# A hybrid decoder layer: the stick-breaking projections in pairs of units by seven block products instead of eight

## The chip, the cores and the metric

The kernel runs on one core of one Trainium2 chip. The metric is device time in microseconds of one execution; two runs of the kernel before took 2079.24 and 2085.99 us, their median is 2082.61 us. Five engines work on their own queues, each in the order in which its instructions stand: TensorE (PE, with its weight loads as PEld), VectorE (DVE), ScalarE (ACT), GpSimd (POOL) and SyncE (SP, which issues nearly all transfers).

## The reference, cut to what matters

Sequence 1024, model width 2048, float32, one layer:

```python
h = rmsnorm(h_res, g_pre[i])
u = h @ w_in[i]                       # 2048 x 7184, split into nine groups of columns
(gq, gk, gv, g_gate, g_lr, sq, sk, sv, s_gate) = jnp.split(u, offsets, axis=-1)
log_a = jax.nn.log_sigmoid(g_lr @ w_a2[i] + b_a[i]) / GLA_TAU
o_gla = gla_chunked(...)              # 4 heads, keys 128 wide, values 256 wide, chunked recurrence
o_gla = rmsnorm(o_gla, g_gla_head[i]).reshape(B, S, D_GLA) * jax.nn.silu(g_gate)
o_sb = stick_breaking(heads(sq), heads(sk), heads(sv))   # 8 heads, 128 wide, strictly causal
o_sb = o_sb.transpose(0, 2, 1, 3).reshape(B, S, D_SB) * jax.nn.silu(s_gate)
mix = jnp.concatenate([o_gla, o_sb], axis=-1) @ w_out[i]
h_res = h_res + rmsnorm(mix, g_post[i])
gate = jax.nn.sigmoid(h_res @ w_ple_gate[i] + b_ple_gate[i])
h_res = h_res + gate * (p[i] @ w_ple_proj[i])
```

In stick-breaking, per query t and earlier key s, A[t,s] = sigmoid(z_ts) times the product of (1 - sigmoid(z_tj)) over the keys j between s and t; z is query times key over sqrt(128).

## The kernel before

**Splitting.** Every operand of a large product is split into two parts, `hi` (an ACT copy that rounds to the matmul's type) and `lo` (a DVE subtraction), and a product is three matmuls: hi with x-hi, lo with x-hi, hi with x-lo. All activations lie with the model dimension on the 128 partitions and tokens along the free axis, in two halves of 512 tokens (`hf` 0 and 1). The normed input x stands split in SBUF as 16 blocks of 128 rows for each half (`x_act[hf][k]`, tiles `ah`, `al`), stored two blocks wide in 16 places.

**Stages.** (1) Load and split x; the first two units run beside it. (2) A unit is 128 columns of `w_in`: `dense` loads four weight tiles of 128x512 (`wload`, `L126`: `raw` by the SP queue, then `split`), and runs 16 blocks x 3 matmuls x 2 halves = 96 matmuls of 128x512 into two PSUM banks called `dn`; at the end the result is taken out on DVE times the row norm `rstd` (`u<-dn,rstd`, `v<-dn,rstd`). First come the 16 units of the four GLA heads, then the 24 units of the eight stick-breaking heads (key, query, value of each). (3) The gate columns (`w_gate`), the output product (`w_out`) and the last gate (`w_g`) are each done as a 2x2 block product by seven block products instead of eight, with sums of x and of the weights; sums of x (`S1` to `S4`) are made in `x_sums`, put to memory and loaded back when a place in SBUF comes free.

**Small products.** `small_product` is a block product: 8 blocks of x by one 1024x128 block of weights, 24 matmuls, from two half loads of weights of 128x512. In the kernel before 16 of them run between the last unit and the wide stages, which use `product` with weights loaded 128x1024.

**Background work.** The chunked recurrence (`gla`) and the stick-breaking attention (`sb`) are generators. After every 6 matmuls of the dense work `step()` moves the generators on; `rate` and `pace` say how often. `sb` makes per head twelve score rows: matmuls into `z`, two sigmoids on ACT (`X<-z`, `E<-z`), the causal mask on POOL (`affine_select`, line 597), a running product on DVE (`L603`), a product (`L608`), an ACT copy and a transposing transfer by SP (`X<-E`, then `E<-X`), eight steps (`L1`) later a DVE copy that regroups (`L618`, `v<-E`) and a split (`s`), and eight steps (`L2`) later the product with the values into banks `o` and `t`. Values are turned the same way (`turn`) and split.

**Order.** The code is written in one order; a scheduler with priorities sets the order on each queue (`high_priority(offset=700)` draws the weights ahead, 300 the evacuations). All waits are semaphores that the scheduler derives from the tiles; a pool's number of buffers limits how far ahead a load can stand. Weights have `raw` 2 and `hi`, `lo` 4 buffers each; one pair of `hi`, `lo` feeds 24 matmuls in `dense` and 12 in `small_product`.

Of the kernel before, what the change touches and what calls it, by code (L numbers as in the profile page):

```python
# [18 lines left out]
P = 128  # L19
# [17 lines left out]
def unit_offsets():  # L37
    offs = []
    for h in range(GLA_HEADS):
        offs += [OFF_GK + P * h, OFF_GQ + P * h, OFF_GV + 2 * P * h, OFF_GV + 2 * P * h + P]  # L40
    for h in range(SB_HEADS):
        offs += [OFF_SK + P * h, OFF_SQ + P * h, OFF_SV + P * h]
    return offs
# [4 lines left out]
RATE_SB = 0.9  # L48
W3 = 4
V_MID, V_END, VW = ("X", "X"), ("E", "E"), 3  # L50
L1, L2, PERIOD = 8, 8, 5
W = 2 * HT
# [3 lines left out]
RATE_TAIL = 1.1  # L56
LAST_11 = 4
PACE_QKV, PACE_TAIL = 15, 4
# [3 lines left out]
def layer(ctx, tc, xT, w_in, w_gate, w_lr, w_a2, b_a, g_pre, g_head, w_out, g_post,  # L62
# [17 lines left out]
    w_open = tc.tile_pool(name="w", bufs=4, side="right")  # L80
# [40 lines left out]
    lo_eng = [V]  # L121

    def wload(src):
        n = src.shape[-1]
        with tc.high_priority(offset=700):
# [4 lines left out]
            dma(raw[:, :n], src)  # L130
# [34 lines left out]
    pace = [0, PACE_QKV]  # L165
# [45 lines left out]
    pair = {}  # L211
    acc = {}
    lr_ps = {0: ps("t"), 1: ps("o")}
    first = [{hf: ps("dn") for hf in HALVES} for _ in range(2)]
    with tc.tile_pool(name="start", bufs=1) as sp:
# [21 lines left out]
        for q in range(4):  # L237
            w = [wload(w_in[n, q]) for n in range(2)]
            for kk in range(4):
                k = 4 * q + kk  # L240
                sl = slice(kk * P, (kk + 1) * P)
                for hf in HALVES:
# [7 lines left out]
                    x_act[hf][k] = (ah, al)  # L250
                    A.activation(ah, raw, AF.Copy, scale=gpre_s[:, k:k + 1])  # L251
# [27 lines left out]
    keep = ctx.enter_context(tc.tile_pool(name="keep", bufs=1, reuse_waits="tile"))  # L279
    with tc.tile_pool(name="att", bufs=1, reuse_waits="tile") as ap:  # L280
        BUFS = {"u": 12, "E": 2, "X": 2, "s": 2, "q": 1, "v": 1, "b": 1, "st": 2, "o": 1, "eb": 4}
        GLA_BUFS = {"a2": 1, "a2h": 1, "a2c": 1, "lr": 1, "kt": 1, "o2": 1, "mask": 1}
        SB_BUFS = {"E2": 2, "s2": 2, "X2": 1}
        own = [tc.tile_pool(name="gla", bufs=1, reuse_waits="tile")]
        own.append(own[0].__enter__())

        def to_sb():
            own[0].__exit__(None, None, None)
            own[0] = tc.tile_pool(name="sb", bufs=1, reuse_waits="tile")
            own[1] = own[0].__enter__()  # L290

        def at(tag, shape=(P, HT), dt=F32):
            pool, bufs = (ap, BUFS[tag]) if tag in BUFS else (own[1], {**GLA_BUFS, **SB_BUFS}[tag])
# [10 lines left out]
        gap(const, 224)  # L304
# [15 lines left out]
        def evac_turned(dst, parts):  # L320
            def go(hf, p):
                vt = at("v")
                V.tensor_tensor(vt, p, rstd[hf], op=ALU.mult)
                if parts == 1:
                    dst[hf] = at("u")
                else:
                    dst[hf] = (at("u", dt=F32R), at("u", dt=F32R))
                urgent.append(turn(vt, dst[hf], parts))
# [10 lines left out]
        def turn(vt, dst, parts):  # L339
            w = turn_by_dma(vt, HT, V_MID[parts - 1], V_END[parts - 1])  # L340
            for _ in range(VW):
                yield 1
            full = dst if parts == 1 else at("o")
# [405 lines left out]

# [633 lines left out]
```

## Time and profile before

| | |
|---|---|
| median of two runs | 2082.61 us |
| span of the profiled execution, first to last instruction | 2075.1 us |
| PE busy | 2060.6 us (99%), 9712 matmuls |
| DVE busy | 1481.9 us (71%) |
| ACT busy | 874.1 us (42%) |
| POOL busy | 112.0 us (5%) |
| transfers | 352.81 MB, mean 170 GB/s |
| granted TensorE clock | 1.000 |

The page gives the profiled execution by its span; a time of its own stands nowhere, so the median is set beside the span: 7.5 us lie between them. In the page's groups of instructions the first number is the busy time in us, the second the mean of one instruction in ns; then follows the idle time of the engine just before these instructions and what ended most of it. A window's row gives, for each engine, the busy time in that stretch and the number of instructions in brackets, then the granted clock, the mean busy share of the 16 DMA engines and the rate. The share of busy time is no bound by itself: matmuls overlap.

### The profile page before, as it was taken

The numbers are of one execution on the slowest core, as the hardware profiler recorded it, in microseconds if no ns is written. First come the engines' busy times: TensorE is split into PE (matmuls) and PEld (weight loads), VectorE is DVE, ScalarE is ACT, GpSimd is POOL, SyncE is SP. The second block draws the span as 40 slices with busy tenths as digits, with TensorE's granted clock in tenths as the row PEclk, the third lists the DMA queues.
The fourth block names the chain that finished last, engine by engine and source line by source line (L and its number), as shares of the span: only waits on it lengthen the run. The fifth ranks groups of instructions, "written<-read, shape, count | busy, mean of one in ns | idle before, by whom it ended". The sixth has DMA issues, their size and how long they took to land.

```text
span 2075.1 us, 26732 instructions
## 1 busy us (share of the span) xinstructions
PE 2060.6 (99%) x9712; PEld 1706.3 (82%) x9712; DVE 1481.9 (71%) x2243; ACT 874.1 (42%) x1390; POOL 112.0 (5%) x229
## 2 busy tenths in 40 slices
PE   9999999999999999999999999999999999999998
PEld 6788888888888888888888788888888888888887
DVE  8657777676766676666567677788778687886765
ACT  7333334333454554555447423344233334423322
POOL 4100000000011011101001000000000000000000
PEclk9999999999999999999999999999999999999999
DMA  6222222232243344443326798888978486886752
GB/s 219 69 67 78 82 78 82 66 87 67 62 126 88 106 107 108 113 105 97 84 79 156 213 328 295 306 298 303 335 283 269 163 313 229 307 292 210 243 190 98
DMA packets 229700, 352.81 MB, mean 170 GB/s; under 512 B 124336, under 2 KB 129344, under 8 KB 229568
## 3 DMA queue, kind: packets, MB, share of 16 engines
q1 hardware_dynamic: 228960, 349.00, 53.2%
q10 hardware_dynamic: 576, 2.10, 0.3%
q8 instruction: 76, 1.25, 0.2%
q14 instruction: 56, 0.46, 0.1%
q0 software_dynamic: 32, 0.01, 0.0%
HBM read 249.85 MB, written 73.92 MB: 156 GB/s over the span
## 4 chain that ended last, share of the span: by engine, by line
PE 90%; DVE 3%; DMA 3%; issue 2%; ACT 1%; SPq 0%; POOL 0%; DVEq 0%; ACTq 0%; POOLq 0%
PE dn L101 79%; PE z L101 5%; PE t L101 3%; PE o L101 3%; DMA E<-X 1%; DMA xraw<-xT 1%; DVE rstd L235 0%; DMA u<-xT 0%; DVE lo L114 0%; DVE al L252 0%; DVE X L603 0%; DVE E L608 0%; DMA raw<-w_gate 0%; ACT hi L113 0%; ACT ah L251 0%
## 5 line engine op out<-in xcount | busy, mean ns | idle before, releaser
L101 PE MATMUL dn<-ah,hi 128*128 128x512 f32 x1408 | 561.7, 399 | 2.3 <-ACT u L736 1.9
L101 PE MATMUL dn<-ah,lo 128*128 128x512 f32 x1408 | 549.6, 390 | 0.2 <-DVE lo L114 0.2
L101 PE MATMUL dn<-al,hi 128*128 128x512 f32 x1408 | 549.4, 390 | 0.0
L101 PE MATMUL dn<-ah,wl 128*128 128x512 f32 x1216 | 473.4, 389 | 0.0
L101 PE MATMUL dn<-al,wh 128*128 128x512 f32 x1216 | 473.1, 389 | 0.0
L101 PE MATMUL dn<-ah,wh 128*128 128x512 f32 x1216 | 473.1, 389 | 0.0
L101 PEld LDWEIGHTS dn<-ah,hi 128*128 128x128 f32 x1408 | 265.0, 188 | 60.2 <-issue 3.6
L101 PEld LDWEIGHTS dn<-al,hi 128*128 128x128 f32 x1408 | 264.3, 188 | 57.6 <-DVE al L252 0.4
L101 PEld LDWEIGHTS dn<-ah,lo 128*128 128x128 f32 x1408 | 265.2, 188 | 48.1 <-DVE lo L114 0.5
L113 ACT ACTIVATE wh<-wr 128x1024 fp32r<-128x1024 f32 x152 | 159.4, 1055 | 268.1 <-PE dn L101 168.9
L101 PEld LDWEIGHTS dn<-ah,wl 128*128 128x128 f32 x1216 | 228.3, 188 | 48.7 <-DVE wl L114 1.2
L101 PEld LDWEIGHTS dn<-al,wh 128*128 128x128 f32 x1216 | 228.3, 188 | 47.3
L101 PEld LDWEIGHTS dn<-ah,wh 128*128 128x128 f32 x1216 | 228.3, 188 | 47.3
L114 DVE TENSOR_TENSOR wl<-wr,wh 128x1024 fp32r<-128x1024 f32 x152 | 185.0, 1218 | 7.0 <-ACT wh L113 6.7
L113 ACT ACTIVATE hi<-raw 128x512 fp32r<-128x512 f32 x192 | 119.7, 625 | 153.4 <-PE dn L101 137.9
L114 DVE TENSOR_TENSOR lo<-raw,hi 128x512 fp32r<-128x512 f32 x192 | 134.7, 703 | 59.6 <-ACT hi L113 59.5
L333 ACT ACTIVATE X<-E 128x256 uint16<-128x256 uint16 (+2 forms) x96 | 81.0, 844 | 142.8 <-DVE E L608 70.2
L603 DVE TENSOR_TENSOR_SCAN X<-X 128x128 f32<-128x128 f32 (+2 forms) x96 | 97.8, 1019 | 14.4 <-POOL X L597 13.0
L618 DVE COPY v<-E 128x512 uint16<-128x512 uint16 (+1 forms) x160 | 64.1, 430 | 48.5 <-DMA E<-X 45.3
L114 DVE TENSOR_TENSOR s<-v,s 128x512 fp32r<-128x512 f32 (+1 forms) x82 | 52.6, 642 | 61.1 <-ACT s L113 60.9
L884 DVE TENSOR_TENSOR wr<-wr,wr 128x1024 f32<-128x1024 f32 x48 | 58.7, 1223 | 49.4 <-issue 15.1
L881 DVE TENSOR_TENSOR wr<-wr,wr 128x1024 f32<-128x1024 f32 x48 | 58.7, 1224 | 47.5 <-DMA wr<-w_g 34.0
(246 smaller groups left out, 2292.6 us busy)
## 6 DMA issues: line engine op xcount, KB each, us to landing
raw<-w_in SPq DMA_DIRECT2D x160, 256.0 KB, 2.7
wr<-w_g SPq DMA_DIRECT2D x64, 512.0 KB, 4.4
wr<-w_out SPq DMA_DIRECT2D x56, 512.0 KB, 4.8
wr<-w_gate SPq DMA_DIRECT2D x40, 512.0 KB, 5.2
g_d<-wr SPq DMA_DIRECT2D x32, 512.0 KB, 3.8
wr<-g_d SPq DMA_DIRECT2D x32, 512.0 KB, 4.5
ar<-h_d SPq DMA_DIRECT2D x28, 512.0 KB, 4.9
ar<-og_d SPq DMA_DIRECT2D x25, 512.0 KB, 5.3
```

Source lines behind the costliest of these rows:

```text
L101: PE.matmul(o, lhsT, rhs, start=start, stop=stop)
L113: A.activation(hi, src, AF.Copy)
L114: (eng or V).tensor_tensor(lo, src, f(hi), op=ALU.subtract)
L333: A.activation(pl.rearrange("p (two n) -> p two n", two=2), src.bitcast(U16)[:, :2 * n].rearrange("p (n two) -> p two n", two=2), AF.Copy)
L603: V.tensor_tensor_scan(rev, rev, rev, initial=kq[:, n:n + 1], op0=ALU.mult, op1=ALU.bypass)
L618: V.tensor_copy(to[:, :, :m, j], w[:, :, 2 * g:2 * g + m])
L881: V.tensor_tensor(dst, a, b, op=ALU.add)
L884: V.tensor_tensor(dst, a, b, op=ALU.subtract)
```

## The change

The 24 stick-breaking units become 12 pairs of 128 columns each. For a pair, the 2048 x 256 weights are seen as 2x2 blocks of 1024 x 128, and x as 2x2 blocks of 1024 rows by 512 tokens; the four results (two units x two halves) come from seven block products in place of eight. The sums of x are made earlier (`x_sets`, from the third unit on), stored already split, and whole sets of x are loaded back into the four places of x during the stage (`load_set`, `swap`). The sums of weights are formed on DVE in a chain tile (`ch<-ch,raw`). The results are no longer taken out of PSUM into SBUF for the heads: they are copied to a tile `pt`, written to memory (`kqv_d`) by SP for a first group of products and added to it by POOL transfers with `accum_op=add` for the second, and each head loads its keys, queries and values when it starts. They are stored without the row norm; keys and values are multiplied by `rstd` on loading, and the queries' norm goes into the scale of the sigmoids (`rq`, for which eight small transposes are added). The gate columns are done the same way: `by_waves` gives four of the seven products, and a last loop the other three, in place of the former gate stages. Half of the regrouping copies of the attention (`L618`) go from DVE to ACT (`regroup`). The output product and the last gate stay as they are.

```diff
-RATE_SB = 0.9
+RATE_SB = 1.0
+Q1, V0, V1, NEXT_Q, NEXT_K = 8, 3, 14, 30, 33
-LAST_11 = 4
-PACE_QKV, PACE_TAIL = 15, 4
+RATE_TAIL = 1.0
+PACE_X, PACE_SET = 5, 2
+ACCUMULATE, REGROUP = False, 1
+BATCHES = ((0, 1, 2), (3, 4, 5), (6, 7))
...
+        def regroup(j, dst, src):
+            if j >= REGROUP:
+                A.activation(dst, src, AF.Copy)
+            else:
+                V.tensor_copy(dst, src)
...
+            def fetch(h, what, hf):
+                if (h, what, hf) not in fetched and h in sb_ready:
+                    fetched[h, what, hf] = t = at("u")
+                    dma2(t, kqv_d[h][what][hf])
...
-                    split(kh[hf], kl[hf], kp[hf])
+                    raw = take(h, 0, hf)
+                    kh[hf], kl[hf] = at(tag, dt=F32R), at("u", dt=F32R)
+                    V.tensor_tensor(raw, raw, rstd[hf], op=ALU.mult)
+                    split(kh[hf], kl[hf], raw)
...
+            tp = ps("z")
+            for c in range(4):
+                PE.transpose(ch(tp, c), ch(rstd[hf], c), idn)
...
+        def load_set(name, slot):
+            got = []
+            for i, (hf, kp) in enumerate(home[slot]):
+                pair = act_wide(hf, kp)
+                for d, t in zip(sx_d[name][i], pair):
+                    with tc.issue_after(last_load[0]):
+                        dma2(f(t), d)
+                    yield 1
+                got.append(pair)
+            sets[name] = parts(got)
...
+        def wt(tag, bufs, dt=F32):
+            return w2.tile([P, HT], dt, tag=tag, name=nm(tag), bufs=bufs)
+        def begin(i, src):
+            chain[i] = []
             for q in range(2):
+                t = wt("ch", 6)
+                last_load[0] = dma(t, part(src, q)).ins
+                chain[i].append(t)
+
+        def extend(i, src):
+            for q, t in enumerate(chain[i]):
...
+                raw = wt("raw", 2)
+                last_load[0] = dma(raw, part(src, q)).ins
+                V.tensor_tensor(t, t, raw, op=ALU.add)
+
+        def small_product(name, i, p):
+            while name not in sets:
+                assert beside
+                advance(beside)
+            a = sets[name]
+            for q in range(2):
+                with tc.high_priority(offset=700):
+                    hi, lo = wt("hi", 3, F32R), wt("lo", 3, F32R)
+                    split(hi, lo, chain[i][q])
...
+        def onto(dst, t, first):
+            if first:
+                dma2(dst, t)
+            else:
+                G.dma_start(dst, t, accum_op=ALU.add)
+
+        def kept(p, scale=1.0):
+            t = wt("pt", 4)
+            A.activation(t, p, AF.Copy, scale=scale)
+            return t
...
+        def by_waves(items, first, weight, at_d, swaps, mid=None):
+            upper, fifth = {}, {}
+            names = ("A11", "s1", "S2", "A22")
+            blocks = ((0, 0), (0, 1), (1, 1), (1, 0))
...
+                with early():
+                    (begin if s == 0 else extend)(i, weight(i, *blocks[s]))
+                p = ps("dn")
+                small_product(names[s], i, p)
+                if x == len(items) - 1 and names[s] in swaps:
+                    swap(names[s], swaps[names[s]])
+                with soon():
+                    if s == 0:
+                        upper[i] = kept(p)
+                        onto(at_d("c11", i), upper[i], first)
+                    elif s == 1:
+                        fifth[i] = p
+                    else:
+                        V.tensor_tensor(upper[i], p, upper[i], op=ALU.add)
+                    if s == 2:
+                        t = wt("pt", 4)
+                        V.scalar_tensor_tensor(t, fifth[i], -1.0, upper[i], op0=ALU.mult, op1=ALU.subtract)
+                        for m in ("c12", "c22"):
+                            if at_d(m, i) is not None:
+                                onto(at_d(m, i), t, first)
+                    elif s == 3:
+                        onto(at_d("c21", i), upper[i], first)
+
+        def by_stages(items, first, weight, at_d, swaps):
+            for m in ((2, 3, 7) if first else (3, 7, 2)):
+                name = {2: "A12", 3: "S4", 7: "S3"}[m]
...
+        to_2, to_1 = {"A11": "S4", "s1": "S3", "S2": "A12"}, {"A12": "A11", "S4": "s1", "S3": "S2"}
+        def sb_items(stage, first, b, swaps={}):
+            stage(range(3 * b, 3 * b + 3), first, lambda i, kh, nh: w_sb[i, kh, nh], sb_d, swaps)
+            pace[1] = PACE_SET
+            if not first:
+                sb_ready.update({2 * b: True, 2 * b + 1: True})
+                rate[1] = RATE_SB
+
+        sb_items(by_waves, True, 0)
+        sb_items(by_waves, True, 1, to_2)
+        sb_items(by_stages, False, 0)
+        sb_items(by_stages, False, 1)
+        sb_items(by_stages, True, 2)
+        sb_items(by_stages, True, 3, to_1)
+        sb_items(by_waves, False, 2)
+        sb_items(by_waves, False, 3)
...
+        for js in BATCHES[:-1]:
+            gate_batch(js)
...
+    gate_batch(BATCHES[-1], {"A11": "A12", "s1": "S3", "S2": "S4"}, to_wide)
...
+            p = product(need("A12"), w2_)
+            gate(j, 0, p, part(p11, j), add)
...
+            p = product(need("S3"), w7)
+            gate(j, 1, p, v(j), lambda z, p, c: sub(z, c, p))
+            gate(8 + j, 1, p, u(j), add)
+            p = product(need("S4"), w3)
+            gate(8 + j, 0, p, u(j), add)
```

Two places of the order show what moves. The first is DVE in the middle of the attention. In the kernel before: `lo` is a weight part, `X` the running product, `E` the score row, `v` and `s` the regrouped weights of the attention, `st` a query, `u<-u,b` a key's split.

```order
L603 SCALAR_TENSOR_TENSOR X_7818<-X_7818 128x512
L114 TENSOR_TENSOR st_8017<-u_7716,st_8017 128x128
L608 TENSOR_TENSOR E_7819<-E_7819,X_7818 128x512
L603 SCALAR_TENSOR_TENSOR X_7839<-X_7839 128x512
L114 TENSOR_TENSOR lo_8081<-raw_8079,hi_8080 128x512
L608 TENSOR_TENSOR E_1634_7840<-E_1634_7840,X_7839 128x512
L114 TENSOR_TENSOR u_7980<-u_7426,b_7979 128x512
```

Of the kernel after, DVE in the attention, during a wave of block products; `ch` is a chain of weights, `pt` a result on its way to memory:

```order
L122 TENSOR_TENSOR lo_9118<-ch_8687,hi_9117 128x512
L657 SCALAR_TENSOR_TENSOR X_9028<-X_9028 128x256
L895 TENSOR_TENSOR ch_8687<-ch_8687,raw_9229 128x512
L895 TENSOR_TENSOR ch_8527<-ch_8527,raw_9332 128x512
L953 TENSOR_TENSOR pt_8609<-dn_8973,pt_8609 128x512
L122 TENSOR_TENSOR lo_9171<-ch_8612,hi_9170 128x512
L956 SCALAR_TENSOR_TENSOR pt_9071<-dn_8804,pt_8609 128x512
L661 COPY eb_9038<-X_9028 128x1
L662 TENSOR_TENSOR E_2006_9029<-E_2006_9029,X_9028 128x256
```

Between the attention's instructions there stood one weight split; now there stand splits, chain sums and sums of results. The second place is POOL at the same spot. Before, only the masks of the score rows and the ones beside them:

```order
L595 MEMSET X_7505 128x1
L597 AFFINE_SELECT X_7470<-X_7470 128x128
L597 AFFINE_SELECT E_7471<-E_7471 128x128
L597 AFFINE_SELECT X_7505<-X_7505 128x128
L597 AFFINE_SELECT E_1563_7506<-E_1563_7506 128x128
```

After, on POOL, with the adding transfers of the results:

```order
L922 DMA kqv_d<-pt_9071 128x512 x2
L649 MEMSET X_9250 128x1
L922 DMA kqv_d<-pt_9222 128x512 x2
L651 AFFINE_SELECT X_9250<-X_9250 128x128
L651 AFFINE_SELECT E_9251<-E_9251 128x128
```

Adding transfers now stand ahead of masks in POOL's queue.

More of the change, by code (lines that the diff above doesn't have):

```diff
@@ L303, in layer @@
         pick = const.tile([P, 2], F32, name="pick")
-        gap(const, 224)
+        rq = [const.tile([P, 8], F32, name=f"rq{i}") for i in range(2)]
+        gminus = const.tile([P, KT], F32, name="gminus")
+        gap(const, 96)
+        V.tensor_scalar(gminus, gpre_s, -1.0, None, op0=ALU.mult)
         V.tensor_copy(pick, sel[:, P:P + 2])
@@ L662, in layer @@
         sb_ready = {}
+        kqv_d = [[[dram.tile([P, HT], F32, name=f"kqv{h}{i}{hf}_d") for hf in HALVES] for i in range(3)]
+                 for h in range(SB_HEADS)]
         def norm_first(hf):
@@ L716, in x_sums, with swap @@
                 keep("S4", k, a12)
+                store_plain()
                 yield 1
+        def load_set(name, slot):
[3 more added lines that the diff above has]
+                for d, t in zip(sx_d[name][i], pair):
+                    with tc.issue_after(last_load[0]):
+                        dma2(f(t), d)
+                    yield 1
+                got.append(pair)
+            sets[name] = parts(got)
+        def swap(old, new):
+            sets.pop(old, None)
+            slot = place.pop(old)
+            place[new] = slot
+            beside.append(load_set(new, slot))
@@ L808, in keep_11 @@
-        def keep_11(j, new):
-            def go(p):
-                t = new()
-                V.tensor_tensor(t, p, part(u1_s[j // 2], j) if j < 6 else u1_s[j], op=ALU.add)
-                dma2(part(c11_d[j // 2], j), t)
-            return go
-        while beside:
-            advance(beside)
-        rate[1], pace[1] = RATE_TAIL, PACE_TAIL
-        beside.append(x_set("S2", 1))
-        for j in range(8):
-            small_product(x_act[0][:8], w_gate[0, 0, j], keep_u1(j))
-        while beside:
-            advance(beside)
@@ new lines, in layer, with gate_batch @@
+        sb_items(by_waves, True, 0)
[6 more added lines that the diff above has]
+        sb_items(by_waves, False, 3)
+        g_d = {m: [dram.tile([P, W], F32, name=f"{m}g{i}_d") for i in range(4)] for m in ("c11", "c12", "c21")}
+        def gate_batch(js, swaps={}, mid=None):
+            by_waves(js, True, lambda j, kh, nh: w_gate[kh, nh, j],
+                     lambda m, j: part(g_d[m][j // 2], j) if m in g_d else None, swaps, mid)
@@ L835, in layer @@
[L835 to L849 removed]
+        att_open.__exit__(None, None, None)
@@ L858, in state @@
         def state(which):
-            return [act.tile([P, W], F32, tag=f"{which}0_{kp}", name=nm("st")) for kp in range(4, 8)]
+            return [act.tile([P, W], F32, tag=f"{which}{hf}_{kp}", name=nm("st")) for hf, kp in home[0]]
         def to_slot(s, i, raw):
@@ L1069, in layer @@
-        drain()
-        job(fill("A11", 0, plain(og_d[0])))
-        for j in range(8):
-            with ahead():
-                w = wsplit(wload2(w_gate[1, 1, j]))
-            p = product(sets["S4"], w)
-            gate(8 + j, 0, p, v(j))
-        drain()
+                w2_ = wsplit(wload2(w_gate[1, 0, j]))
+                t3, b22 = wload2(w_gate[0, 1, j]), wload2(w_gate[1, 1, j])
+                add(t3, t3, b22)
+                w7, w3 = wsplit(t3), wsplit(b22)
+                if j % 2 == 0:
+                    with tc.issue_after(last_load[0]):
+                        dma2(st_v[j // 2], g_d["c21"][j // 2])
+                        dma2(st_u[j // 2], g_d["c12"][j // 2])
```

355 lines of the change are left out of this document (193 added, 162 removed).

## Prediction

> **What bounds the kernel now.** First the page's head and its chain of what ended last.
>
> ```profile
> span 2075.1 us, 26732 instructions
> PE 2060.6 (99%) x9712; PEld 1706.3 (82%) x9712; DVE 1481.9 (71%) x2243; ACT 874.1 (42%) x1390; POOL 112.0 (5%) x229
> ...
> PE 90%; DVE 3%; DMA 3%; issue 2%; ACT 1%; SPq 0%; POOL 0%; DVEq 0%; ACTq 0%; POOLq 0%
> ```
>
> PE has 90% of the chain. What one of its matmuls is worth has to be read twice: from the groups, and from the same chain in order of time, where the dense product runs undisturbed.
>
> ```profile
> L101 PE MATMUL dn<-al,hi 128*128 128x512 f32 x1408 | 549.4, 390 | 0.0
> ...
> 1172.74 344.35 PE dn L101 x1519
> ```
>
> One matmul lasts 390 ns, but 1519 in a row take 344.35 us, which is 226.7 ns each: they overlap, and only the interval counts for the span. The page "Perfetto Trace Analysis" of the Trainium skill, section "Identifying the Most-Contended Engine", says the same of busy time: for TensorE it is no measure of the way to the limit, because the instructions are pipelined. By busy time the 288 matmuls below would be worth 112 us, by the interval 65; the trace decides for the interval.
>
> Then the windows, by stage: the GLA heads, the attention, its last 50 us, the passage to the wide stages, a wide stretch, and the one with the most DVE work.
>
> ```profile
> 150.00:550.00 400.00, 399.44 (x2072) 333.16 (x2071) 290.81 (x579) 154.06 (x266) 14.37 (x13) 1.00 0.26 75
> 570.00:1150.00 580.00, 578.97 (x2809) 487.73 (x2807) 387.63 (x746) 308.92 (x607) 65.97 (x189) 1.00 0.42 107
> 1100.00:1150.00 50.00, 50.00 (x243) 42.21 (x242) 39.14 (x75) 34.47 (x70) 7.19 (x19) 1.00 0.63 163
> 1150.00:1180.00 30.00, 27.09 (x130) 22.05 (x129) 20.12 (x34) 15.46 (x27) 0.00 (x0) 1.00 0.69 204
> 1200.00:1500.00 300.00, 300.00 (x1325) 248.40 (x1324) 233.13 (x228) 104.89 (x107) 0.00 (x0) 1.00 0.88 310
> 1750.00:1800.00 50.00, 50.00 (x223) 41.40 (x222) 45.07 (x48) 23.13 (x29) 0.00 (x0) 1.00 0.91 312
> ```
>
> PE is the bound in every stage. In the attention DVE is busy for 67% and ACT for 53%: there is room, and the question is how much of it the change uses up. The passage shows the first loss: 2.9 us of 30.
>
> **The change, part by part.**
>
> *Matmuls.* The order holds 7872 matmuls into `dn` before and 7584 now: 24 units of 96 are 2304, 12 pairs of 7 products of 24 are 2016. 288 x 0.2267 us = 65.3 us, all on the path. The eight transposes of the norm cost between 0.06 us each (a quarter of a 512-column interval) and their full duration in the nearest row:
>
> ```profile
> L492 PE MATMUL t<-c,E 128*128 128x128 f32 x32 | 4.9, 274 | 0.3 <-DVE E L390 0.3
> ```
>
> that is 0.5 to 2.2 us; I take 1.
>
> *DVE in the attention.* Its work has to fit beside a shorter PE. In the new order the first score row stands at `dn` matmul 2346 (before: 1968), the last product with values at 4224 (4122). In the window above 733 of 2809 matmuls are not `dn`: (580 - 2076 x 0.2267) / 733 = 0.149 us each. The new stretch is then 1878 x 0.2267 + 768 x 0.149 = 540 us of PE, the old one 603. For DVE the interval counts too, not the duration:
>
> ```profile
> L114 DVE TENSOR_TENSOR lo<-raw,hi 128x512 fp32r<-128x512 f32 x93 | 63.8, 686 | 29.0 <-ACT hi L113 28.8
> L603 DVE TENSOR_TENSOR_SCAN X<-X 128x512 f32<-128x512 f32 x47 | 60.4, 1285 | 7.1 <-POOL X L597 6.0 <-ACT X L592 1.0
> L618 DVE COPY v<-E 128x512 uint16<-128x512 uint16 x123 | 54.3, 461 | 44.9 <-DMA E<-X 41.8 <-ACT X L333 1.8
> ...
> 844.35 0.68 DVE L608 TENSOR_TENSOR E<-E,X 128x512 f32<-128x512 f32 x1
> 844.95 0.68 DVE L114 TENSOR_TENSOR u<-u,b 128x512 fp32r<-128x512 f32 x1
> 845.56 0.69 DVE L114 TENSOR_TENSOR u<-u,q 128x512 fp32r<-128x512 f32 x1
> 846.16 0.28 DVE L114 TENSOR_TENSOR st<-u,st 128x128 fp32r<-128x128 f32 x1
> ...
> 848.36 0.65 DVE L618 COPY v<-E 128x512 uint16<-128x512 uint16 x2
> ```
>
> Back to back, an operation of 0.69 us starts every 0.61 us and a copy of 0.46 every 0.33. Counted in the new stretch: 157 weight splits, 98 chain sums, 36 sums of results, 30 products with `rstd`, 30 splits of values and keys: 351 x 0.61 = 214; running products 90 (durations less 0.085, by length); score rows 46; splits of the regrouped rows 44; 80 regrouping copies 26 (half went to ACT); the rest 27. Together 447 of 540 us, 83%. The same count for the old stretch gives 382 of 603, 63%, where the window shows 67%, so I read 87%. In the two full gate batches the count is 146 of 166 us, 88%, read as 92%. Lower bound of the price: nothing, since at 1750 DVE is busy for 45.07 of 50 us and PE loses nothing. Upper bound: in no 50 us of attention did DVE pass 78% (39.14); held to that, 447 x 1.05 / 0.78 = 602, 62 us too long. The buffers speak for something between: a pair `hi`, `lo` now feeds 12 matmuls, 2.7 us, and there are 3 (before 24 and 4, 21.8 us), so a DVE that stands still for more than some 8 us is felt. It does stand still, in order:
>
> ```profile
> DVE s L114 <- ACT s L113: 62.7, 47, 4.0
> ...
> DVE v L618 <- DMA E<-X: 45.3, 37, 3.0
> ...
> DVE X L603 <- POOL X L597: 13.0, 24, 1.8
> ```
>
> These waits are up to 4 us; queued behind them now are the weight splits with the shorter lead. I take 14 us: a tenth of the two batches' 166 us missing (at 92% wanted and near 84% had) and nothing earlier.
>
> *ACT.* It gains one `hi` per 12 matmuls, the copies to `pt` and half the regrouping.
>
> ```profile
> 814.27 0.62 ACT L113 ACTIVATE hi<-raw 128x512 fp32r<-128x512 f32 x1
> 814.79 0.29 ACT L113 ACTIVATE st<-u 128x128 fp32r<-128x128 f32 x1
> ```
>
> At 0.52 us per 512 columns the same count is 382 of 540 us, 71%. Nothing of its own.
>
> *Transfers.* By the shapes in the order 458 MB are moved, 105 more: results written, added and read, eleven sets of x of 4 MB loaded, more of x stored. In the attention stretch 113 MB instead of 62 (107 GB/s x 580 us). At the rate and share of 1200 to 1500 us (310 GB/s at 0.88) the extra 51 MB are 145 us of all engines; with 0.42 x 580 = 244 that is 389 of 540, 0.72. A wide stretch at 0.88 loses nothing. But SP's queue is one:
>
> ```profile
> SPq L130 <- DVE lo L114: 364.2, 114, 14.9
> ...
> raw<-w_in SPq DMA_DIRECT2D x160, 256.0 KB, 2.7
> wr<-w_gate SPq DMA_DIRECT2D x40, 512.0 KB, 5.2
> E<-X SPq DMA_TRANSPOSE x128, 2.7
> ```
>
> SP already stands before weight loads until a buffer comes free; there the transposes queue behind it, and now also loads of results and sets. A set comes in eight loads, two per product; two are late by this count: S2 before the third wave (six of eight issued when its first product is due) and S4 in the passage. Each costs between nothing and one landing, 5.2 us; the passage itself loses 2.9 us today and will move more (17 MB in some 40 us, where 310 GB/s gives 12). Bounds 0 and 15; I take 6.
>
> *POOL.* 48 adding transfers stand in its queue, 36 of them in the attention, among the masks that the running products wait for. Only one transfer of POOL is in the trace:
>
> ```profile
> L597 POOL TENSOR_SCALAR_AFFINE_SELECT E<-E 128x128 f32<-128x128 f32 x64 | 36.0, 563 | 21.1 <-ACT E L593 20.2
> ...
> L108 POOL DMA_DIRECT2D c<-g_pre x1 | 0.7, 702 | 0.8 <-POOLq L1378 0.8
> ```
>
> 36 x 0.7 = 25 us on an engine busy for 66 of 580: hidden by the eight steps between score row and regrouping. Low end 0, high end 36 x 2.7 us (a landing each, nearest row above) = 97. I take 3, being nearest to the row of POOL itself.
>
> *GLA heads.* The sums of x move here: 368 us of DVE by count instead of 311, so 0.73 becomes 0.86 of the window. I take 1 us, by the row at 1750; 0 to 10. The wide gate loop that replaces the gate stages has as many products; nothing.
>
> Sum, against the span: 2075.1 - 65.3 + 1 + 14 + 6 + 3 + 1 = 2034.8. The median of the runs lies 7.5 above the span, so 2042 us, 1.9% less. The forecast's own range, with its terms at a third and at double, is 2025 to 2067.
>
> **The rivals.**
>
> *Everything is hidden* (0.15). For it: PE loses nothing at 1750 with DVE at 90% and DMA at 0.91. Against: there one weight tile feeds 24 matmuls and nothing chains DVE to ACT, POOL and transposes. 2082.6 - 64.3 + 2 = 2020.
>
> *DVE takes PE's place as the bound* (0.20). The waits in order keep it at 78 to 80% in the attention; the loss is 45 to 62 us in place of 14. For it: the 63 us behind ACT, the 45 behind transposes. Against: those waits were idle time that cost nothing, and shrink when the queue is full. 2042 - 14 + 53 = 2081, no change.
>
> *POOL's adding transfers hold the rest up* (0.10); this one ends slower. An adding transfer waits at the head of POOL's queue for its `pt`, the masks wait behind it, the running product behind the masks, and DVE's weight splits behind that; ACT, too, waits for one of four `pt` to be read out. At 2.5 us each, near a landing, 36 are 90 us: 2042 - 3 + 90 = 2129. It decides (2% slower, 2124) from (2124 - 2039) / 36 = 2.4 us each. Against: POOL is 11% busy and the masks have steps in hand. The page "SBUF — State Buffer" of the Trainium skill, section "SBUF: two separate sides", speaks for it: POOL writes the descriptors of its transfers into SBUF, and a DVE copy in a two-port mode locks it out until it ends. No run here shows it; with a copy of 0.46 us it would be short each time.
>
> **How the numbers follow.** Forecast 0.55, and the rivals 0.15, 0.20, 0.10. 2% is about what a measurement of this kernel can tell from no change; it lies at 2041 and 2124. About half of the forecast's weight lies under 2041: faster 0.15 + 0.28 = 0.43. Same 0.27 + 0.20 = 0.47. Slower 0.10. The range goes from 2016 (nothing lost, and the two or three us that the passage and the attention lose today) to 2092 (DVE as the bound at its upper price); it leaves out the slower rival and a little at the bottom.
>
> **What would show it.** Right: PE's records near 9430 and its busy share still 97% or more; DVE at 83 to 90% of the attention's windows; one late wait of PE on DVE `lo` or on a reloaded `ah` at the third wave and in the passage. Wrong: PE windows of the attention under 46 of 50 us (DVE the bound, if its own windows stay under 42); long waits of DVE on POOL, or of ACT on `kqv_d<-pt` (the slower rival); PE's loss in the GLA heads.

## The result, and the profile after

The changed kernel takes 2179.14 us (median of two runs, 2178.91 to 2179.38) against 2082.61: the ratio is 1.0465, with a 95% interval of 1.0424 to 1.0506. It is 4.6% slower; 2042 was predicted. The profiled execution has a span of 2177.7 us, 102.6 more than before. First the page's head and its chain of what ended last.

```profile
span 2177.7 us, 27224 instructions
PE 2060.4 (95%) x9432; PEld 1672.4 (77%) x9432; DVE 1576.0 (72%) x2408; ACT 998.9 (46%) x1622; POOL 158.3 (7%) x277
...
PE 26%; DVE 9%; DMA 8%; issue 3%; ACT 2%; SPq 0%; POOL 0%; DVEq 0%; ACTq 0%
```

280 PE records are gone (288 matmuls less, eight transposes more; 9430 was foreseen), yet PE is as long busy as before: a matmul's record gets longer under a slow clock (628 ns in the stretches where it is halved, 390 before) and still counts as busy. In the chain PE has 26% where it had 90%. The windows of the GLA heads, the attention, its densest part, the passage, a wide stretch, and the one with the most DVE work (engines in the order PE, weight load, DVE, ACT, POOL; then granted clock, DMA share, GB/s):

```profile
150.00:550.00 400.00, 391.91 (x2010) 322.25 (x2009) 311.01 (x612) 166.27 (x291) 17.45 (x13) 1.00 0.48 160
690.00:1330.00 640.00, 577.46 (x2620) 464.15 (x2621) 467.81 (x840) 417.12 (x791) 97.60 (x226) 0.96 0.71 179
900.00:1110.00 210.00, 179.42 (x792) 143.02 (x792) 149.60 (x267) 123.42 (x231) 36.95 (x76) 0.94 0.77 183
...
1330.00:1360.00 30.00, 26.96 (x114) 21.71 (x113) 19.03 (x26) 9.72 (x15) 0.00 (x0) 0.89 0.92 326
1400.00:1700.00 300.00, 294.45 (x1278) 241.90 (x1277) 233.89 (x231) 107.58 (x110) 0.00 (x0) 0.98 0.84 295
1850.00:1900.00 50.00, 50.00 (x223) 41.39 (x222) 44.48 (x48) 23.15 (x29) 0.00 (x0) 1.00 0.90 309
```

In the attention PE is busy for 90%, DVE for 73% and ACT for 65%: no engine is full. The clock, 1.00 in every window before, is 0.94 in the middle. The wide window with DVE at 89% still loses nothing. PE's waits, with their total, count and longest:

```profile
PE dn L109 <- ACT hi L121: 32.2, 16, 11.3
PE dn L109 <- DVE lo L122: 29.9, 38, 4.4
PE z L109 <- DVE st L122: 10.3, 5, 4.9
PE dn L109 <- DMA al<-S32l_d: 7.4, 1, 7.4
PE dn L109 <- ACT u L858: 5.8, 1, 5.8
```

**Where the 102.6 us are.** For a sum, each interval from the start of one matmul to the start of the next is set against the median interval of the same two shapes in the trace before. By that measure the matmuls themselves went from 2039.8 to 1975.3 us, 64.5 less; what is lost beyond them went from 27.6 to 194.6 us, 167.0 more; 167.0 - 64.5 = 102.5. Of the 194.6 us, 35.9 are lost in intervals that lie wholly in stretches in which the clock was halved. The table gives the same by place, with the runs that follow in its columns, each by its one profiled execution (two executions of a kernel lie up to 12 us apart, so 2 or 3 us in a row say nothing); a stretch runs from one `dn` matmul, counted from the start, to another, and the first column is what its matmuls take by those medians.

| us, from and to `dn` matmul | matmuls | changed | ring | store | nochain | noadd | noset | allout |
|---|---|---|---|---|---|---|---|---|
| GLA units, 192 to 1536 | 370.3 | 392.4 | 393.0 | 394.9 | 392.5 | 391.9 | 376.7 | 378.3 |
| first block products, to 2346 | 211.7 | 234.5 | 221.1 | 222.8 | 226.9 | 238.8 | 229.8 | 215.4 |
| stages of products, to 2976 | 178.1 | 211.7 | 208.1 | 198.7 | 209.6 | 224.7 | 212.1 | 192.4 |
| second waves, to 3552 | 163.3 | 218.0 | 206.5 | 192.0 | 200.4 | 200.8 | 207.7 | 172.3 |
| gate batches, to 4224 | 192.1 | 214.9 | 217.4 | 217.8 | 201.1 | 200.9 | 217.0 | 200.7 |
| passage and gate loop, to 4896 | 154.0 | 170.7 | 171.3 | 167.9 | 162.3 | 163.1 | 155.4 | 153.8 |

The kernel before lost 8.7 us in its whole attention and took 378.0 us for the GLA units.

The largest single loss is at the first pair of heads. POOL's timeline (start, duration, and in brackets the idle time before, with "issue" where nothing that the profile shows ended it), then SP's wait in that place, then DVE's in the whole run (total in us, count, longest):

```profile
667.25 0.87 POOL L922 DMA_DIRECT2D kqv_d<-pt  x1 [4.03 <-issue]
671.58 0.89 POOL L922 DMA_DIRECT2D kqv_d<-pt  x1 [3.46 <-issue]
676.18 0.88 POOL L922 DMA_DIRECT2D kqv_d<-pt  x1 [3.71 <-issue]
680.52 0.89 POOL L922 DMA_DIRECT2D kqv_d<-pt  x1 [3.47 <-issue]
```

```profile
SPq L581 <- DMA kqv_d<-pt: 19.2, 2, 18.7
```

```profile
DVE u L596 <- DMA u<-kqv_d: 20.4, 3, 16.1
```

POOL issues one adding transfer each 4.4 us, and in between waits for nothing that the profile shows of another engine. SP stands 18.7 us before the load of the first keys, with weight loads behind it; DVE waits 16.1 us for those keys; ACT's `hi` behind that is the 11.3 us wait of PE above; and from within that wait on, the clock is halved for 20.5 us.

Later the masks stand behind such a transfer. At 719.28 us POOL issues one, at 725.34 the next, and the mask after it starts at 725.90; DVE has waited 7.2 us for that mask, PE 4.4 us for the `lo` behind it, and at 727.4 the clock is halved again. What DVE's running products waited for masks, in the changed kernel and in the run ring below:

```profile
DVE X L657 <- POOL X L651: 29.5, 34, 7.2
```

```profile
DVE X L655 <- POOL X L649: 12.2, 37, 2.0
```

The kernel before has 13.0 us of it, 1.8 at the longest.

### The profile page after: what moved, and what is told of

The parts are those of the page before. It is cut to its first block, busy times and chain, and to the rows that moved or that the text cites. A ratio compares the mean times of both kernels' runs of the same rounds, so it can differ in the third digit from the quotient of the medians.

```text
span 2177.7 us, 27224 instructions
## 1 busy us (share of the span) xinstructions
PE 2060.4 (95%) x9432; PEld 1672.4 (77%) x9432; DVE 1576.0 (72%) x2408; ACT 998.9 (46%) x1622; POOL 158.3 (7%) x277
## 5 line engine op out<-in xcount | busy, mean ns | idle before, releaser
L109 PE MATMUL dn<-ah,lo 128*128 128x512 f32 x1440 | 577.3, 401 | 30.6 <-DVE lo L122 29.9
L109 PE MATMUL dn<-al,wh 128*128 128x512 f32 x1088 | 425.3, 392 | 9.4 <-DMA al<-S32l_d 7.4
L109 PE MATMUL dn<-ah,wh 128*128 128x512 f32 x1088 | 426.0, 392 | 3.6 <-ACT ah L121 3.5
L109 PE MATMUL dn<-ah,wl 128*128 128x512 f32 x1088 | 426.2, 392 | 2.2 <-DVE wl L122 2.2
L122 DVE TENSOR_TENSOR lo<-ch,hi 128x512 fp32r<-128x512 f32 x232 | 159.5, 687 | 85.9 <-ACT hi L121 85.1
L121 ACT ACTIVATE hi<-ch 128x512 fp32r<-128x512 f32 x232 | 144.0, 622 | 94.5 <-PE dn L109 90.0
L657 DVE TENSOR_TENSOR_SCAN X<-X 128x128 f32<-128x128 f32 (+2 forms) x96 | 97.8, 1018 | 31.9 <-POOL X L651 29.5
L895 DVE TENSOR_TENSOR ch<-ch,raw 128x512 f32<-128x512 f32 x144 | 98.6, 692 | 14.8 <-DMA raw<-w_sb 9.2
L1062 DVE TENSOR_TENSOR wr<-wr,wr 128x1024 f32<-128x1024 f32 x40 | 48.9, 1223 | 42.2 <-DMA wr<-w_g 31.1
L554 ACT ACTIVATE v<-E 128x512 uint16<-128x512 uint16 (+1 forms) x80 | 53.4, 668 | 48.1 <-DVE s L122 47.0
L121 ACT ACTIVATE ah<-ar 128x1024 fp32r<-128x1024 f32 x40 | 42.4, 1060 | 68.9 <-DVE ar L1065 31.3
```

The lines of the kernel that those rows point to most:

```text
L109: PE.matmul(o, lhsT, rhs, start=start, stop=stop)
L121: A.activation(hi, src, AF.Copy)
L122: (eng or V).tensor_tensor(lo, src, f(hi), op=ALU.subtract)
L554: A.activation(dst, src, AF.Copy)
L657: V.tensor_tensor_scan(rev, rev, rev, initial=kq[:, n:n + 1], op0=ALU.mult, op1=ALU.bypass)
L895: V.tensor_tensor(t, t, raw, op=ALU.add)
```

## The experiments

Each run is compared with the kernel before on the same chip. The theories when they began: the operands come late because DVE and ACT work through their queues in order (A); POOL's adding transfers (B); the reloads of x (C); the chain's additions (D).

**POOL's adding transfers.**

```diff
 # store: the second contribution
-                G.dma_start(dst, t, accum_op=ALU.add)
+                dma2(dst, t)
 # ring: the memory for descriptors, and two unused paddings out
-    gap(const, 192)
...
-        gap(const, 64)
...
-                   dynamic_dma_scratch_size=512)
+                   dynamic_dma_scratch_size=1024)
 # late_ring: as ring, and issued in the middle of the product that follows
+                    if k == 5:
+                        flush()
...
-                G.dma_start(dst, t, accum_op=ALU.add)
+                pending.append((dst, t))
 # poolstore: as ring, and
-                G.dma_start(dst, t, accum_op=ALU.add)
+                G.dma_start(dst, t)
```

store: 

> The second group of block products no longer adds to the stored keys, queries and values with POOL's transfers: the same bytes are stored by SP, so the second contribution replaces the first (the attention works on incomplete keys, queries and values). Theory A (the operands of the products come late because DVE and ACT work through their queues in order, among the attention's work): only what hangs on the adding transfers at the first pair of heads goes, PE's 11.3 us pause at 685 us, the 20.5 us at half clock behind it, and a few short waits of DVE on POOL: 20 to 30 us less than 2179, so 2150 to 2160. Theory B (POOL's adding transfers, one every 4.5 us, hold the whole stretch up): 80 us or more of the 135 us of waits go, 2100 or less.

ring: 

> The same computation; the scratch memory in which POOL's transfers are described is 1024 bytes a partition for 512, and two unused paddings of 192 and 64 bytes make room for it. If the size of that memory paces the adding transfers, they are issued less than 4.5 us apart in a row and the first pair of heads starts earlier: theory A gives 10 to 25 us less than 2179; theory B, by which these transfers hold everything up, 40 us less or more. If the pace is the transfer's own, no change: 2174 to 2184.

late_ring: 

> The whole computation, with 1024 bytes of scratch memory (2154.6 us without more), and each adding transfer is issued in the middle of the product that follows (some 18 matmuls, 4 us, later), when its result has long been read out, so that it no longer stands at the head of POOL's queue with the attention's masks behind it. If the remaining 26 us of the adding transfers are POOL's order: 12 to 25 us less, 2130 to 2143. If they are the transfers themselves (their reads and writes, the loads that wait for them): 2150 to 2158.

poolstore: 

> With 1024 bytes of scratch memory, POOL issues the second contributions as plain stores, which do not add (the second contribution replaces the first, so the attention works on incomplete keys, queries and values). If the adding is the price of the remaining 26 us: as with SP's stores, 2126 to 2136. If it is POOL's issue and its descriptors: as with the larger memory, 2149 to 2158.

Measured: store 2128.88 us (ratio 1.0224, 1.0155 to 1.0294), ring 2154.63 (1.0348, 1.0318 to 1.0378), late_ring 2152.67 (1.0341, 1.0311 to 1.0371), poolstore 2132.98 (1.0240, 1.0180 to 1.0299). The adding transfers cost 50 us, twice what A expected and less than B. By the table they cost where they stand: of the 48, 12 stand in the first block products (11.7 us less without them), 12 in the stages (13.0) and 24 in the second waves (26.0), some 1.05 us each; the other rows move by 3 us or less. Half of it is the memory for descriptors. In ring, POOL's timeline at the same place, where several issues follow each other at once, and what POOL waits for is the result (its lines stand two lower there):

```profile
645.41 1.79 POOL L920 DMA_DIRECT2D kqv_d<-pt  x2 [4.65 <-ACT pt L924]
650.83 1.76 POOL L920 DMA_DIRECT2D kqv_d<-pt  x2 [3.63 <-ACT pt L924]
656.32 1.76 POOL L920 DMA_DIRECT2D kqv_d<-pt  x2 [3.73 <-ACT pt L924]
```

The 60.7 us that POOL waited for "issue" are gone, and 24.5 us of the time. With them go the long waits for masks (29.5 to 12.2 us above), so in this half a part is POOL's order; the runs don't part it from the pace of the transfers. Of the other half, POOL's order is no part (late_ring is the same as ring within their spreads), nor is the issue by POOL as far as these runs resolve it (poolstore and store lie 4 us apart, and each scatters by 10). What remains is the adding itself, about 22 us, as sure as that scatter lets it be. Issue to landing, first in ring, then in poolstore (the last number):

```profile
kqv_d<-pt POOLq DMA_DIRECT2D x48, 256.0 KB, 5.3
```

```profile
kqv_d<-pt POOLq DMA_DIRECT2D x48, 256.0 KB, 3.8
```

An adding transfer of 256 KB lands in 5.3 us, a plain one from the same queue in 3.8. The Trainium skill, "DMA: Bandwidth & Descriptors", section "Rules for kernel authors", says that an accumulating transfer reads its destination and writes it later; the longer landing agrees.

**The sets of x.**

```diff
 # noset: the sets are what stands in the slots, and x_sets isn't started
-                pair = act_wide(hf, kp)
...
-                        dma2(f(t), d)
...
+                got.append(x_wide[hf, kp])
...
-            if u == 2:
-                beside.append(x_sets())
 # xcompute: as noset, but x_sets runs, without its stores
```

noset: 

> The sets of x are neither computed, stored nor reloaded: every product takes the operands that stand in its slot since the start (the results are not those of the block products). Theory A: the 14 us in the stage of the GLA units and some 15 us of the waits at the passage and at the two reloads go, 2145 to 2155. Theory C (the reloads fill the DMA engines, whose share is 0.97 in the windows of the second reload, and so hold the weights up): 80 us or more go, 2100 or less.

xcompute: 

> The sets of x are computed, from the same loads, but neither stored nor reloaded (products take what stands in the slots, as in the run without sets at 2132.2). If the 14 us in the stage of the GLA units are DVE's and ACT's work, that stage ends where it does in the changed kernel (435.7 us) and the time is 2143 to 2150. If they are the stores (28 MB, 56 issues on SP beside the weights), it ends near 422 and the time is 2128 to 2137.

Measured: noset 2132.21 (1.0240, 1.0200 to 1.0281), xcompute 2142.82 (1.0294, 1.0264 to 1.0324). Of the 47 us, 15.7 lie in the GLA units and 15.3 in the passage and the gate loop, as A had it; what goes beyond A's 2145 to 2155 lies in the second waves, 10.3, beside the reloads that go on there, and in the first products, 4.7. With the sets computed but not stored the GLA units take 388.9 us: 12 of their 15.7 us are the loads of x and the work of DVE and ACT on it, 3.5 the stores. C, as one cause of everything, falls.

**The chain, and DVE's and ACT's work.**

```diff
 # nochain: no load and no addition
-            for q, t in enumerate(chain[i]):
+            for q, t in enumerate([]):
 # noadd: only the loads
-                V.tensor_tensor(t, t, raw, op=ALU.add)
 # nochain4: as nochain, and
-                    hi, lo = wt("hi", 3, F32R), wt("lo", 3, F32R)
+                    hi, lo = wt("hi", 4, F32R), wt("lo", 4, F32R)
 # rg0: all regrouping on ACT
-ACCUMULATE, REGROUP = False, 1
+ACCUMULATE, REGROUP = False, 0
 # acc
-ACCUMULATE, REGROUP = False, 1
+ACCUMULATE, REGROUP = True, 1
-                   dynamic_dma_scratch_size=512)
+                   dynamic_dma_scratch_size=1792)
 # acc_late: as acc, the results' adding transfers issued as in late_ring
```

nochain: 

> The chain of weight blocks isn't continued: a product takes the block that its chain began with, so 144 loads of 0.25 MB and 144 additions on DVE of about 0.4 us (59 us in all) are left out, and the products use the wrong sums. Theory A: some of the late lo tiles come in time, 20 to 40 us less than 2179, 2140 to 2160. Theory D (the additions, which stand ahead of a block's split in DVE's queue and wait for two raw tiles, are what makes the operands late): 80 us or more, 2100 or less.

noadd: 

> The chain's 144 loads stay, the 144 additions on DVE go (the products use the block with which the chain began). If it is DVE's work and its order that the chain costs (theory A), nearly all of the 53 us go as without the chain: 2125 to 2140. If it is the loads (DMA share, the two raw tiles, SP's order), most of it stays: 2160 to 2180.

nochain4: 

> Without the chain (its 144 loads and additions are left out, the products use the block with which it began, as in an earlier run at 2126.6), and the room of the two raw tiles goes to the split weights: four hi and four lo tiles for three, so DVE and ACT may be one quarter of a block (12 matmuls, 2.7 us) further ahead of TensorE. If the lead is what makes single late operands cost time (the theory: the queues of DVE and ACT stand still for 2 to 5 us now and then, and a lead of two tiles doesn't cover it), 20 to 35 us less than 2126.6: 2092 to 2107. If the operands are late because the queues are too full on the mean, the lead changes little: 2118 to 2128.

rg0: 

> The changed kernel, and the regrouping of both rows of a pair on ACT, where DVE has done the first: 80 copies of 467 ns (37 us) leave DVE, with their waits for the turned tiles (36 us), and ACT gets 80 of about 670 ns. If it is DVE's work and its waits in order that make the operands late (theory A), 15 to 30 us less than 2179: 2149 to 2164. If it is the order of either engine alike, ACT's own splits come late in their place: 2170 to 2190.

acc: 

> The whole computation, with 1792 bytes of scratch memory; the 144 additions of the chain are made by adding transfers of POOL, straight into the chain's tiles, and DVE loses 99 us of work. If the chain's price is DVE's load, and POOL's queue bears 192 transfers: 2154 less 25 to 40, 2115 to 2130. If POOL's queue is what breaks (144 more issues of 0.9 us, each waiting for the split of the block before it, with masks behind): 2190 or more.

acc_late: 

> As the one before, with the adding transfers of results issued in the middle of the following product. 5 to 20 us less than that one if POOL's order is what it costs, else the same within 5.

Measured: nochain 2126.57 (1.0213, 1.0184 to 1.0243), noadd 2153.91 (1.0343, 1.0306 to 1.0381), nochain4 2122.16 (1.0189, 1.0151 to 1.0228), rg0 2184.85 (1.0490, 1.0460 to 1.0521), acc 2201.61 (1.0576, 1.0546 to 1.0607), acc_late 2195.33 (1.0546, 1.0475 to 1.0617). The addition's row in the changed kernel, beside the split's:

```profile
L122 DVE TENSOR_TENSOR lo<-ch,hi 128x512 fp32r<-128x512 f32 x232 | 159.5, 687 | 85.9 <-ACT hi L121 85.1
L895 DVE TENSOR_TENSOR ch<-ch,raw 128x512 f32<-128x512 f32 x144 | 98.6, 692 | 14.8 <-DMA raw<-w_sb 9.2 <-DMA raw<-w_gate 3.5
```

It lasts 692 ns, not the 0.4 us of the expectation. Without the chain 53 us go, between the ranges of A and D. Where the attention is dense, in the second waves and the gate batches, leaving out only the additions does as much as leaving out the loads too (200.8 and 200.4, 200.9 and 201.1): there it is DVE's work, or its waits for the loaded block, which go with the addition (14.8 us in the row above). In all, noadd gains only 25, between its two ranges, because at the first pair of heads it is worse (238.8 and 224.7 in the second and third rows). There one wait of PE on `hi` is 20.1 us, behind a wait of DVE of 24.3 us for the first keys; why they come later than in the changed kernel no run shows.

The lead is not the cause, as far as a run without the chain tells: a fourth pair of split tiles changed 4 us where 20 to 35 were expected. Nor is it DVE alone: rg0 takes work from DVE and gives it to ACT, and the time does not fall. Its window of the densest part, to be set against the third row above:

```profile
900.00:1110.00 210.00, 177.84 (x777) 141.74 (x776) 142.14 (x243) 139.80 (x259) 36.88 (x74) 0.92 0.75 181
```

DVE 7 us less, ACT 16 more, and 777 matmuls for 792. And POOL couldn't take the additions (what it waited for in acc, the total, the count and the longest):

```profile
POOL ch L891 <- DVE lo L122: 277.4, 96, 33.4
```

Each addition there must wait until the block before it has been split, at the head of a queue in which the attention's masks stand too. acc_late lies 6 us under acc, less than its own two executions lie apart, so it decides nothing.

**Smaller groups.**

```diff
 # two_ring: ring, and
-BATCHES = ((0, 1, 2), (3, 4, 5), (6, 7))
+BATCHES = ((0, 1), (2, 3), (4, 5), (6, 7))
-                t = wt("ch", 6)
+                t = wt("ch", 4)
-                    hi, lo = wt("hi", 3, F32R), wt("lo", 3, F32R)
+                    hi, lo = wt("hi", 4, F32R), wt("lo", 4, F32R)
 # sb_items likewise in groups of two;  two_ring_rg0: and REGROUP = 0
```

two_ring: 

> The whole computation: the block products in groups of two units for three, so that four chain tiles do for six and the split weights get four hi and four lo tiles for three; and the scratch memory of POOL's transfers is 1024 bytes as in the run at 2154.6. If the lead is what is short, 25 to 45 us less than 2154.6: 2110 to 2130. If it is not, no more than 10 us less: 2145 to 2158.

two_ring_rg0: 

> As before in groups of two with four split tiles and 1024 bytes of scratch, and the regrouping of both rows on ACT: if both DVE's work and the lead count, 10 to 20 us less than the one with DVE's regrouping, 2095 to 2115; if ACT gets late in DVE's place, the same or more, 2120 to 2140.

Measured: two_ring 2167.62 (1.0408, 1.0352 to 1.0464), two_ring_rg0 2180.39 (1.0469, 1.0439 to 1.0499); both slower than ring and than every range expected. PE's waits in two_ring:

```profile
PE z L109 <- DVE st L121: 14.1, 18, 2.0
PE z L109 <- ACT E L645: 11.1, 6, 3.9
PE dn L109 <- DMA ah<-S32h_d: 9.5, 1, 9.5
PE z L109 <- DVE u L121: 6.8, 6, 1.5
```

The weights are in time now (PE waits 5.4 us in all for `lo`, 26.1 in ring), and the attention's own operands (`z` is the tile of the scores) are late in their place: the longer lead only changes which operand waits. It is not all of the loss: by the stretches of the table two_ring takes 231.0 us for the first block products and 189.3 for the passage and gate loop, 10 and 18 more than ring. Of the 18 us, 5 are matmuls that fall into that stretch; in both, sets of x come late, with the 9.5 us above as the longest wait.

**All three, and no attention.**

```diff
 # allout: store, noset and nochain together
 # noatt, and bnoatt likewise in the kernel before
-        jobs.append(sb())
...
+                    dma2(part(o_d[hf][4 + h], dv), ot[dv])
```

allout: 

> The three cuts at once: second contributions stored and not added, no sets of x made or reloaded, no chain of weight blocks. Apart they took 50, 47 and 53 us off 2179. If these are three costs with a place each, they add up: 2029, 2020 to 2040, with the waits of PE back near those of the kernel before. If they are one cost (a queue that is too full, which each of them relieves), the sum falls short: 2055 or more.

noatt: 

> The changed kernel without the attention of the stick-breaking heads (the GLA results are stored in its place; the projections, their block products and stores, the sets and the gates stay). To be set against the same cut in the kernel before. Theory A (the operands come late because the attention's work stands among the splits): 40 to 55 us less than that one, that is the 64.5 us of matmuls less the stage of the GLA units (12 us) and the passage to the gate's loop. The rival (the block products are late by themselves: three weight tiles ahead, two raw tiles, the reloads): 15 us less or nothing.

bnoatt: 

> The kernel before without the attention of the stick-breaking heads (the GLA results are stored in its place). TensorE is busy nearly all the time there, and the attention's own matmuls of this kernel are what goes, so the theories agree on it: 1800 to 1860, with TensorE at 98% or more. It is the measure for the cut of the changed kernel.

Measured: allout 2047.33 (0.9831, 0.9796 to 0.9867), noatt 1936.63, bnoatt 1961.08. The three cuts give 132 us, 88% of their sum of 150, between the two outcomes expected: three costs, with an overlap of 18. The densest part in allout:

```profile
900.00:1110.00 210.00, 205.08 (x989) 168.75 (x988) 160.62 (x293) 150.72 (x285) 27.86 (x72) 1.00 0.48 133
```

989 matmuls for 792 (the same time, so a later part of the work), the clock back at 1.00, and DVE busier than in the changed kernel, though its additions are gone. The pages without the attention, of the changed kernel and of the one before:

```profile
PE 1899.7 (98%) x8664; PEld 1554.0 (80%) x8664; DVE 1296.6 (67%) x1848; ACT 700.3 (36%) x1029; POOL 91.3 (5%) x85
```

```profile
PE 1946.6 (99%) x8944; PEld 1603.5 (82%) x8944; DVE 1217.0 (62%) x1667; ACT 652.1 (33%) x909; POOL 43.9 (2%) x37
```

Without the attention the change is a gain of 24.5 us; with it, a loss of 96.5. So 40 of the 64.5 us are lost without any attention (more than the expected 10 to 25), and 121 us only because the attention runs beside the block products. By the stretches of the table noatt loses 23, 12 and 8 us in the first three and under 1 in each of the others: in the second waves it takes 130.9 us where its matmuls alone take 130.8, with the same additions and adding transfers in them that cost 17 and 26 us beside the attention. In that stretch they have a price only there. bnoatt lies 100 us above its expected range: the attention's 768 matmuls (9712 less 8944) are 121 us, not 220 or more.

## Why the prediction was wrong

The range ended at 2092. The step that failed is the one from work to time: the terms for what the change adds came to 25 us, most of them priced from rows in which nothing was lost, and the runs that take the adding transfers, the sets and the chain out again gain 50, 47 and 53 us apart and 132 together. Of the signs named, the number of PE records came (9432); DVE at 83 to 90% of the attention's windows did not (73%).

- **Matmuls, -65.3 us: right.** 64.5 by the intervals, transposes included.
- **DVE in the attention: the load right, its price wrong.** 447 of 540 us were counted and read as 87%; 467.81 us were measured, 87% of 540. The price was 14 us, and its lower bound came from a wide window with DVE at 90% and no loss. The additions alone cost 31 us in the second waves and gate batches, and with all three suspects gone the attention still loses 32 us (the allout column, rows three to five) where it lost 9. The failed sentence is the one against the second rival, that DVE's waits "were idle time that cost nothing, and shrink when the queue is full". In the second waves DVE was busy for 155.9 of 218.0 us; without additions for 130.1 of 200.8; idle 62 and 71 us. The waits stayed. DVE waits for ACT, ACT for DVE, both for transposes; 37 us of copies moved from one to the other gained nothing (rg0). ACT, given "nothing of its own", was busy for 417 us in the attention where 382 were counted, and DVE's wait for its `hi` is 99.3 us in the whole run (59.5 before). The wide stages have no such chain, so their window said nothing about the attention; the prediction said so itself against the rival "everything is hidden", and took its own lower bound from that window all the same. The argument from the buffers got no support (nochain4, two_ring).
- **POOL, 3 us: wrong.** The cost is 50 us, 1.05 us each by 48. The row taken for it, 0.7 us of issue, is POOL's own time, not the transfer's. The rival's 90 us were nearer than the 3. Its mechanism, masks behind a waiting transfer, is there with 512 bytes of descriptor memory (7.2 us at 726 us, 29.5 us of DVE's waits for 12.2 in ring) and has no part in what remains with 1024 (late_ring); what holds POOL there is less the `pt`, as the rival had it, than the pace of one transfer at a time. What remains with 1024 is the adding and its slower landing. The rule cited for it from the Trainium skill ("SBUF — State Buffer", section "SBUF: two separate sides"), that DVE can lock POOL out while it writes descriptors, got no support: plain stores issued by POOL cost nothing that can be told from SP's.
- **Transfers 6 us, GLA 1: wrong together.** noset takes 47 us off. A late load in the passage came as foreseen (7.4 us on `al<-S32l_d`; 5.2 was the price), though of S3 and not S4, and none of S2 shows among PE's waits. The gate loop behind it and the second waves pay too. The GLA units lost 14 us, beyond the upper bound of 10: again a window with room (DVE from 73 to 78%) was taken for one without a price.
- **The clock: not in the sum at all.** 35.9 us are lost while it is halved, more than all the losses of the sum together.
- **The rivals.** "DVE takes PE's place" named the right place, and its sign came: PE at 45 of 50 us in the attention with DVE at 36.5. Its 53 us were too few, since it stood alone; what came was it, the adding transfers and the sets together, and a halved clock behind the longer pauses. Nor is DVE the bound by itself, at 73%. The forecast added up small terms, most of them priced at a near row without loss.

What stays open: why the last 32 us of the attention are lost when nothing of the three is left (the shorter PE beside the same attention, by the windows, but no run took that alone), and whether a faster version exists. ring and late_ring are the best whole versions here, 24.5 and 26.5 us better than the change and still 3.5 and 3.4% slower than the kernel before.

## What to carry to other kernels

A busy share said nothing here of the price of more work: DVE at 89% cost nothing in a wide stage, and at 73% it came too late in the attention. Where two in-order engines feed each other, count their work and the waits between them against the shorter PE time, and don't borrow the price from a stage without that chain. For a transfer that adds, look at the space between issues and at the landing, not at the issue alone: here it was 0.9 us of POOL, 4.4 us from one to the next, and 1.05 us of the kernel. A longer lead of buffers didn't help here: another operand was late instead.

## What the runs showed of the hardware

**The clock was halved after pauses of about 2 us.** In the changed kernel it falls to 0.50 sixteen times between 65 and 1560 us, for 3.4, 6.8 or once 20.5 us; before, at no time before the end. Windows of the 3.4 us ahead of two such falls, and of what follows each:

```profile
898.10:901.50 3.40, 1.34 (x6) 0.75 (x5) 1.70 (x5) 1.44 (x3) 0.00 (x0) 1.00 1.06 348
901.50:908.30 6.80, 6.30 (x14) 4.71 (x15) 5.88 (x10) 5.30 (x9) 1.36 (x2) 0.50 0.77 260
...
1556.90:1560.30 3.40, 1.38 (x6) 1.05 (x6) 2.46 (x3) 1.00 (x2) 0.00 (x0) 0.99 0.97 392
1560.30:1563.70 3.40, 3.40 (x9) 2.63 (x8) 3.39 (x4) 0.00 (x0) 0.00 (x0) 0.50 1.03 420
```

PE was idle for 2.1 and 2.0 of 3.4 us. In 15 of the 16 cases it was idle for 1.68 us or more of the 3.41 us ahead of the fall, in one for 1.40; on the same grid of 3.41 us no stretch with more than 1.67 us of idle time went without one (in the run acc one with 1.79 did). So about half a stretch of idle time was enough here. A matmul started every 0.427 us under the halved clock and every 0.227 under the full one, so a wait of 2 us can cost another 1.6 (an estimate from these two intervals). The Trainium skill, "TensorE: Matmul & The Clock Gate", section "Part 1: The HAM clock gate", has the stretch of about 3.4 us, and the half rate after at least one idle one; the length agrees, but most of the pauses here were shorter than that, and the measurement decides.

**Adding transfers of POOL went one at a time when their descriptor memory was 512 bytes a partition**, one each 4.4 us; with 1024, two were issued within 1.8 us, and the kernel took 24.5 us less.
